# FFN2's last product: seven half-size products over 20 of 22 feature tiles instead of 16, with token sums, weight parts and residuals in a new order

## The chip, the cores and the metric

The kernel runs on 1 core of one Trainium2 chip. The metric is the device time of one execution in microseconds (us); lower is better. Before the change the median of 3 runs is 1121.24 us (1120.5 to 1123.13).

## The reference, cut to what matters

The program is one layer of a streaming encoder: a half-step SwiGLU feed-forward block (FFN1), a mixer, a second half-step feed-forward block (FFN2), and a final RMS norm. Only the end is touched:

```python
def swiglu(h, w1, w3, w2):
    return (jax.nn.silu(h @ w1) * (h @ w3)) @ w2
...
        x = x + 0.5 * swiglu(rms_norm(x, ffn2_norm[l]), ffn2_w1[l], ffn2_w3[l], ffn2_w2[l])
    return rms_norm(x, final_norm)
```

There are 512 tokens, 1024 model columns and 2816 features, all in float32. The change concerns the product with `w2` (512 x 2816 by 2816 x 1024), the residual add and the final norm.

## The kernel before, in words

**Precision.** Every float32 operand is used as two parts: a high part (`hi`, a cast to the matmul's type, on ACT) and a low part (`lo`, the operand minus the high part, on DVE). One product of two operands is then three matmuls: hi by hi, lo by hi, hi by lo.

**The last product.** The features lie in 22 tiles of 128 (`hh[j]`, `hl[j]`: the two parts of tile j, features on partitions, tokens along the row). A *unit* is two neighbouring feature tiles, with a `w2` block of 128 x 2 x 512 (512 KB) for one half of the columns. A matmul takes 128 tokens of a tile as its stationary side and 512 columns of `w2` as its moving side. `ByTokens.run` (L1879) handles 16 tiles in the Strassen-Winograd way: the features are cut in two halves of 4 units (`NU` = 4, `K2` = 8), the tokens in two halves of 256, the columns in two halves of 512, and seven half-size products stand in for eight. Each of the seven has 4 steps, one a unit (`seventh`, L1974), of 12 matmuls. The other 6 tiles (16 to 21) are multiplied plainly (`plainly`, L1984): 48 matmuls for each pair of tiles.

In the text the seven are M1, M2 (plain tokens of the first half by the two feature halves), M5, M6, M3, M7 (with sums of tokens or of weights) and M4. M5 multiplies by the token sum S1, which is written back over the second half of the tokens of `h`; M6, M3 and M7 multiply by the sums S2, S4 and S3. The results collect in eight PSUM banks: X, Y, Z and W of two banks each. Z holds M5 first; `snap` (ACT, L1998) copies it away (`m5`), and then M3 is added to the same bank. X likewise holds M1, then M1 + M6 (`up`), then M7 and M4.

**Weights.** The sums of weight blocks are made by accumulating transfers: `onto` (L1893) lets GpSimd (POOL) issue a transfer from memory that adds to what lies in the buffer. A buffer of the list `chain` holds B11 (M1), then B11 + B12 (M5), then + B22 (M6), then + B21 (M4). An `onto` must wait until the block's present content has been read by both instructions that make its parts, and the next use must wait until it has landed. Plain loads (`fetch`, L1888) go through SP's queue.

**Order.** Everything is emitted in program order and kept so on each engine. `prep` (L1954) makes the two parts of a weight block: a cast on ACT (L1964) and a subtraction on DVE (through `two`, L1903). There are three pairs of buffers for weight parts, used in turn, so the parts of a step can be made once the step three places before it has read its own. `parts` (L1940) makes the two parts of a token sum for M6, M3 and M7, in three buffers in turn. The token sums are made on DVE by `whole`, `s1` and `s234`. In the order before, all four M5 steps come first, then the four M6, four M3, four M7, one plain step, four M4 and the remaining plain tiles; M6's unit u thus uses the buffer `chain[u]` four places after M5's unit u.

**The end.** Each block of 128 tokens gets its last plain matmuls, the residual (read back from `xtok` in memory to `ys`), the sum of squares and the scaling, one block after another, and is stored.

Engines are written PE (matmuls), PEld (loading of the stationary side), DVE, ACT, POOL and SP.

Of the kernel before, what the change touches and what calls it, by code (L numbers as in the profile page):

```python
# [18 lines left out]
P = 128  # L19
# [4 lines left out]
KF = DFF // P  # L24
DA = 512
# [26 lines left out]
def kernel(  # L52
# [658 lines left out]
    def ffn(nrm, w1, w3, w2, nxt, during=(), first=None, seven=None):  # L711
        with tc.tile_pool(name="hp", bufs=1) as hp:
# [9 lines left out]
            def place_h(j):  # L722
                got = []
                if by_tokens and j < 8:
                    if j == 0:
                        firsts.append(hp.tile([P, 8, 2, T], F32R, name="h0to7"))
                    return [firsts[0][:, j, i] for i in range(2)]
# [1124 lines left out]
    class ByTokens:  # L1852
# [5 lines left out]
        def early(s, sv, nrm):  # L1858
            s.sv, s.nrm = sv, nrm

            def scales():
                ps = bank("rst", pr)
                for b in range(NB):
                    keep(pe.transpose(ps[:, b * P:(b + 1) * P], nrm.rstd[:, b * P:(b + 1) * P], ident[:]))
                keep(act.activation(s.small[:, 0:NB], ps[:, 0:T:P], AF.Copy, scale=0.5))

# [12 lines left out]
        def run(s, hh, hl, h, w2, hp):  # L1879
            H, sc, NU = s.H, s.small, 4  # L1880
# [12 lines left out]
            def onto(to, k0, c):  # L1893
                keep(nc.gpsimd.dma_start(to, part(k0, c), accum_op=ALU.add))
# [4 lines left out]
            def mm(ps, a, b, start=False, stop=False):  # L1899
                keep(pe.matmul(ps if isinstance(ps, bass.AP) else ps[:], a, b, start=start, stop=stop, skip_group_check=True))  # L1900

            def two(to, a, b, op=ALU.subtract):
                keep(dve.tensor_tensor(to, a, b, op=op))  # L1903

            chain = [t[:] for t in s.sv.first_raw]
# [6 lines left out]
            S2, S4 = [fp.tile([P, 2 * NU, H], F32, name=f"s{i}", tag=f"O{i}") for i in range(2)]  # L1912
            S3 = [xp.tile([P, 2, H], F32, name="s3", tag="acc", bufs=2)[:] for _ in range(2)]
            S3 += [fp.tile([P, 2, H], F32, name="s3", tag="sq7")[:], xp.tile([P, 2, H], F32, name="s3", tag="rstd")[:]]
            RA, RB = [None] * NU, [None] * NU

            def whole(u):
                ks = slice(2 * u, 2 * u + 2)
                RA[u], RB[u] = unit("E00", name="ra"), unit("E01", name="rb")
                two(RA[u], f32(h[:, ks, 0]), f32(h[:, ks, 1]), ALU.add)  # L1920
                for k in range(2):
                    kk = 2 * NU + 2 * u + k
                    two(RB[u][:, k], f32(hh[kk]), f32(hl[kk]), ALU.add)

            def s1(u):
                v, to = RB[u][:, :, H:T], [h[:, 2 * u:2 * u + 2, i, H:T] for i in range(2)]
                two(v, RA[u][:, :, H:T], v)
                return lambda: keep(act.copy(to[0], v)), lambda: two(to[1], v, f32(to[0]))

            def s234(u):  # L1930
                ks = slice(2 * u, 2 * u + 2)
                two(S2[:, ks], RB[u][:, :, H:T], RA[u][:, :, 0:H])
                two(S3[u], RA[u][:, :, 0:H], RA[u][:, :, H:T])
                two(S4[:, ks], RB[u][:, :, 0:H], S2[:, ks], ALU.add)
# [5 lines left out]
            def parts(S, u):  # L1940
                hi, lo = spots[turn[0] % 3]
                turn[0] += 1
                src = S[u] if isinstance(S, list) else S[:, 2 * u:2 * u + 2]
# [8 lines left out]
            made, done = [2], [0]  # L1952

            def prep(src, own=None):  # L1954
                n = made[0]
                if own:
                    hi, lo = [unit(t, F32R) for t in own]
                else:
                    made[0] += 1
                    if n % 3 == 2:  # L1960
                        hi, lo = fp.tile([P, 2, T], F32R, name="whi", tag="fg")[:], unit("E30", F32R, "wlo")
                    else:
                        hi, lo = [wp.tile([P, 2, T], F32R, tag=t, name=t, bufs=2)[:] for t in ("whi", "wlo")]
                keep(act.copy(hi, src))  # L1964
                two(lo, src, f32(hi))
                if own:
                    return hi, lo
                wide.append((hi, lo))

            def take():  # L1970
                done[0] += 1
                return wide[done[0] - 1]

            def seventh(banks, left, start=False):  # L1974
                hi, lo = take()
# [8 lines left out]
            def plainly(k0, c, ts, start=False):  # L1984
                hi, lo = take()
# [4 lines left out]
                for k in range(2):  # L1990
                    for t in ts:
                        mm(bank_of[t][c], token(hh[k0 + k], t), lo[:, k])
# [12 lines left out]
            prep(chain[2])  # L2005
            whole(0)
            onto(chain[0], 0, 1)
            onto(chain[1], 2, 1)
            seventh(X, plain_h(0, 0), True)
            prep(chain[3])  # L2010
            onto(chain[2], 4, 1)
            onto(chain[3], 6, 1)
            prep(b21[0])
            cast, rest = s1(0)
            seventh(X, plain_h(2, 0))
            prep(b21[1])
            cast()
            f = [fetch(tags[0], 16, 0)]
            s234(0)
            rest()  # L2020
            seventh(X, plain_h(4, 0))
            prep(b21[2])
            f.append(fetch(tags[1], 16, 1))
            whole(1)
            seventh(X, plain_h(6, 0))
            prep(b21[3])
            f.append(fetch(tags[2], 18, 0))
            cast, rest = s1(1)
            seventh(Y, plain_h(K2, 0), True)
            prep(f[0])  # L2030
            cast()
            f.append(fetch(tags[3], 18, 1))
            s234(1)
            rest()
            seventh(Y, plain_h(K2 + 2, 0))
            prep(f[1])
            x0 = snap(X, "x0", 0)
            whole(2)
            seventh(Y, plain_h(K2 + 4, 0))
            prep(f[2])  # L2040
            cast, rest = s1(2)
            seventh(Y, plain_h(K2 + 6, 0))
            prep(f[3])
            cast()
            s234(2)
            rest()
            plainly(16, 0, (0, 1))
            prep(chain[0])
            onto(chain[0], K2, 1)
            whole(3)  # L2050
            plainly(16, 1, (2, 3), True)
            prep(chain[1])
            onto(chain[1], K2 + 2, 1)
            cast, rest = s1(3)
            plainly(18, 0, (0, 1))
            prep(chain[2])
            cast()
            onto(chain[2], K2 + 4, 1)
            plainly(18, 1, (2, 3))
            rest()  # L2060
            s234(3)
            prep(chain[3])
            onto(chain[3], K2 + 6, 1)
            seventh(Z, plain_h(0, 2), True)
            b22 = [fetch(t, K2 + 2 * u, 1) for u, t in enumerate(("E10", "E11", "E00", "E01"))]
            seventh(Z, plain_h(2, 2))
            left = [parts(S2, 0)]
            prep(chain[0])
            seventh(Z, plain_h(4, 2))
# [149 lines left out]
```

## Time and profile before

| what | value |
|---|---|
| median of 3 runs | 1121.24 us (1120.5 to 1123.13) |
| time of the profiled execution | 1121.77 us |
| span of the profiled execution (first to last instruction) | 1120.1 us |
| mean granted clock of TensorE | 0.999 |
| PE busy | 1108.4 us (99%) |
| DVE busy | 911.0 us (81%) |
| ACT busy | 648.8 us (58%) |
| starts of the first and the last matmul of FFN2's last product | 1002.3 us and 1112.4 us |

A profile comes from one execution. The page gives busy times by engine, the chain of work that ended last and the costliest groups of instructions; further views answer for a stretch of time: the timeline of an engine, who waited for whom, busy time by stretch, and transfers with the time from issue to landing. In a timeline row the columns are start, duration, engine, line, operation, what is written from what, count, and in brackets the engine's idle time before it with what ended that. Matmuls overlap: one lasts 0.389 us, and the next begins before it ends.

### The profile page before, as it was taken

The page shows a single profiled execution, that of the slowest core. Times are in us where ns is not written, and L with a number is a line of the kernel's source. Part 1 is how long each engine was busy: PE and PEld are TensorE (multiplying, and loading weights), DVE is VectorE, ACT ScalarE, POOL GpSimd, SP SyncE. Part 2 cuts the span into 40 slices and gives each one's busy share as a digit, 9 for nine tenths or more (in the row PEclk, how much of TensorE's full clock was granted, in tenths as well). Part 3 has the DMA queues.
Part 4 walks back from the last instruction along what each step waited for, and adds up shares of the span by engine and source line. Part 5 has one row for each costly group of instructions (what it writes and reads, how often), then busy time and mean ns, then how long its engine had stood idle before and what let it go on. Part 6 is the DMA issues. An engine that isn't in the chain of part 4 may idle for free.

```text
span 1120.1 us, 19519 instructions
## 1 busy us (share of the span) xinstructions
PE 1108.4 (99%) x7640; PEld 974.3 (87%) x7640; DVE 911.0 (81%) x1429; ACT 648.8 (58%) x1085; POOL 106.1 (9%) x170
## 2 busy tenths in 40 slices
PE   8999999999999999999999999999999999999997
PEld 7899999998887888888777777788999999998786
DVE  6889999988556888768777677878989999989766
ACT  6646555644335954444879768544766655554554
POOL 2000000010000112321000001112000000001220
PEclk9999999999999999999999999999999999999999
DMA  8433333353344343345222236543344433356792
GB/s 264 126 95 105 113 96 113 95 180 114 113 123 119 83 118 110 116 118 140 68 58 74 86 101 194 158 129 95 104 123 126 120 113 96 114 166 172 172 269 105
DMA packets 198218, 139.55 MB, mean 125 GB/s; under 512 B 10574, under 2 KB 178830, under 8 KB 198126
## 3 DMA queue, kind: packets, MB, share of 16 engines
q1 hardware_dynamic: 185854, 110.77, 33.6%
q0 software_dynamic: 10032, 26.74, 9.2%
q8 instruction: 60, 0.98, 0.4%
q10 hardware_dynamic: 2240, 0.79, 0.3%
q14 instruction: 32, 0.26, 0.1%
HBM read 123.41 MB, written 14.88 MB: 123 GB/s over the span
## 4 chain that ended last, share of the span: by engine, by line
PE 92%; issue 3%; DMA 3%; DVE 1%; POOL 0%; ACT 0%; SPq 0%; DVEq 0%; POOLq 0%; ACTq 0%
PE za L142 23%; PE zc L142 14%; PE pgt L142 8%; PE pd L142 6%; PE pk L142 6%; PE ppj L1702 4%; PE pw L142 4%; PE pq L142 4%; PE tx L1900 3%; PE pb L142 3%; PE pa L142 3%; PE pv L142 2%; PE tz L1900 2%; PE pl L142 1%; DMA raw<-in_ffn_w_dram 1%
## 5 line engine op out<-in xcount | busy, mean ns | idle before, releaser
L133 ACT CAST whi<-raw 128x1024 fp32r<-128x1024 f32 (+2 forms) x93 | 90.0, 969 | 104.2 <-issue 16.6
L134 DVE TENSOR_TENSOR wlo<-raw,whi 128x1024 fp32r<-128x1024 f32 (+2 forms) x93 | 104.4, 1123 | 22.5 <-ACT whi L133 22.2
L142 PE MATMUL zc<-xh,wlo 128*128 128x256 f32 x296 | 83.7, 283 | 0.0
L142 PE MATMUL zc<-xl,whi 128*128 128x256 f32 x296 | 83.7, 283 | 0.0
L142 PE MATMUL zc<-xh,whi 128*128 128x256 f32 x296 | 83.7, 283 | 0.0
L142 PE MATMUL za<-e,wtwo 128*128 128x256 f32 x480 | 64.2, 283 | 0.0
L142 PEld LDWEIGHTS za<-e,wtwo 128*128 128x128 f32 x480 | 59.6, 188 | 0.0
L512 ACT CAST wtwo<-wsum 128x1024 fp32r<-128x1024 f32 x37 | 38.9, 1052 | 31.2 <-PE za L142 31.2
L142 PEld LDWEIGHTS zc<-xh,wlo 128*128 128x128 f32 x296 | 56.7, 191 | 0.0
L142 PEld LDWEIGHTS zc<-xl,whi 128*128 128x128 f32 x296 | 56.7, 191 | 0.0
L142 PEld LDWEIGHTS zc<-xh,whi 128*128 128x128 f32 x296 | 56.6, 191 | 0.0
L142 PE MATMUL pgt<-xh,whi 128*128 128x512 f32 x128 | 53.0, 414 | 0.0
L515 DVE TENSOR_TENSOR wlo<-raw,whi 128x1024 fp32r<-128x1024 f32 x41 | 50.0, 1219 | 2.5 <-ACT whi L512 2.5
L524 DVE TENSOR_TENSOR wsum<-wsum,raw 128x512 f32<-128x512 f32 x74 | 50.9, 688 | 1.2
L524 DVE TENSOR_TENSOR wsum<-raw 128x512 f32<-128x512 f32 x74 | 50.7, 685 | 0.0
L142 PE MATMUL pgt<-xh,wlo 128*128 128x512 f32 x128 | 50.1, 391 | 0.0
L142 PE MATMUL pgt<-xl,whi 128*128 128x512 f32 x128 | 50.0, 391 | 0.0
L512 ACT CAST whi<-wsum 128x1024 fp32r<-128x1024 f32 x37 | 38.8, 1049 | 16.7 <-PE zc L142 13.4
L512 ACT CAST whi<-raw 128x1024 fp32r<-128x1024 f32 x41 | 43.1, 1050 | 8.9 <-PE zc L142 7.9
L598 ACT ACTIVATE fs<-fa 128x512 f32<-128x512 f32 x39 | 24.7, 632 | 38.8 <-DVE fa L631 31.6
L515 DVE TENSOR_TENSOR wlo<-wsum,whi 128x1024 fp32r<-128x1024 f32 x37 | 45.1, 1219 | 0.0
L515 DVE TENSOR_TENSOR wtwo<-wsum,wtwo 128x1024 fp32r<-128x1024 f32 x37 | 45.1, 1218 | 0.0
(693 smaller groups left out, 3604.2 us busy)
## 6 DMA issues: line engine op xcount, KB each, us to landing
raw<-in_ffn_w_dram SPq DMA_DIRECT2D x106, 512.0 KB
raw<-in_w_in_dram SPq DMA_DIRECT2D x40, 512.0 KB
wu<-in_ffn_w_dram SPq DMA_DIRECT2D x18, 512.0 KB
raw<-in_ffn_w_dram POOLq DMA_DIRECT2D x12, 512.0 KB, 8.8
raw<-in_w_out_dram SPq DMA_DIRECT2D x8, 512.0 KB
raw<-in_ffn_w_dram SPq DMA_DIRECT2D x8, 384.0 KB
gsave<-gs SPq DMA_DIRECT2D x9, 256.0 KB
xin<-in_x_dram SPq DMA_DIRECT2D x4, 512.0 KB
```

Source lines behind the costliest of these rows:

```text
L133: marks["wide"] = act.copy(hi[:], raw[:])
L134: marks["rest"] = (eng or dve).tensor_tensor(lo[:], raw[:], hi[:].bitcast(F32), op=ALU.subtract)
L142: mm = pe.matmul(ps, w, x_, start=first and n == 0, stop=last and n == 2, skip_group_check=chain)
L512: keep(act.copy(dst, src))
L515: keep(dve.tensor_tensor(dst, src, f32(hi), op=ALU.subtract))
L524: keep(dve.tensor_tensor(to, a, b, op=ALU.add))
L598: keep(act.activation(sa[:], a_[:], AF.Silu))
L1702: keep(pe.matmul(ps[:], a[:, k, :], y[k][b], start=k == 0 and n == 0, stop=k == NP - 1 and n == 2))
L1900: keep(pe.matmul(ps if isinstance(ps, bass.AP) else ps[:], a, b, start=start, stop=stop, skip_group_check=True))
```

## The change

Ten units of two tiles are now handled by the seven products (`KS` = 10 tiles in each feature half, `NU` = 5), and one pair of tiles (20 and 21, `KP` = 20) plainly. The order of the steps is a list, and a table (`plan`) says what is emitted after each step; `ready(n + 3)` emits the parts for the step three places ahead, after the table's row. The steps are numbered from 0: M1 0 to 4, M2 5 to 9, the plain pair's two steps 10 and 11, M5 and M6 12 to 21, M3 22 to 26, M7 27 to 31, a plain step 32, M4 33 to 37, and the last plain step 38.

M5 and M6 are no longer one behind the other as wholes: units 0, 1, 2 of M5, units 0, 1, 2 of M6, then M5 and M6 of unit 3, then M5 and M6 of unit 4. The token sums of unit 4 are prepared by transfers: `sent` copies the high parts of its four tiles inside SBUF (SP's queue), and `joined` adds the low parts (POOL's queue); the buffers that they use (`r0`, `r1`) become those of `up` and `m5` later. The fifth block of `chain` lies in `E10`. Blocks for M3 and M7 (`b22`) are fetched for units 0 to 2 early, and for units 3 and 4 after step 21, since their buffers `E00` and `E01` hold the token sums until then. The residuals are added by accumulating transfers to the saved results (`x0`, `m5`, `up`), and the token blocks 0 and 1 are finished before the last plain step; only blocks 2 and 3 remain for the end.

Line numbers of the changed kernel differ: `onto` is L1897, `two` L1906, `prep`'s cast L2013, `parts`' cast L1999, `snap` L2041.

```diff
+KS = 10
...
-            K2 = 2 * NU
-            tags = ["E10", "E11", "E20", "E21"]
-            b21 = [fetch(tags[u], K2 + 2 * u, 0) for u in range(NU)]
...
-            seventh(Z, plain_h(2, 2))
-            left = [parts(S2, 0)]
-            prep(chain[0])
-            seventh(Z, plain_h(4, 2))
-            left.append(parts(S2, 1))
-            prep(chain[1])
...
+            chain.append(fetch("E10", 8, 0))
...
+            def sent(u):
+                R[u] = [[xp.tile([P, T], F32, name=f"r{n}{i}", tag=f"x{i}{5 + n}")[:] for i in "hl"] for n in range(2)]
+                for n in range(2):
+                    for k in range(2):
+                        kk = n * KS + 2 * u + k
+                        keep(nc.sync.dma_start(over(R[u][n][k], hh[kk]), f32(hh[kk])))
...
+            K2, KP = KS, 2 * KS
+            b21 = [fetch(t, K2 + 2 * u, 0) for u, t in enumerate(("E11", "E20", "E21"))]
+            order = [("M1", u) for u in range(NU)] + [("M2", u) for u in range(NU)] + [("F", 0), ("F", 1)]
+            order += [("M5", 0), ("M5", 1), ("M5", 2), ("M6", 0), ("M6", 1), ("M6", 2), ("M5", 3), ("M6", 3), ("M5", 4), ("M6", 4)]
+            order += [(m, u) for m in ("M3", "M7") for u in range(NU)] + [("L", 1)] + [("M4", u) for u in range(NU)] + [("L", 0)]
...
+            def ready(n):
+                m, u = order[n]
+                if m in ("M6", "M3", "M7"):
+                    made["left", m, u] = parts({"M6": S2, "M3": S4, "M7": S3}[m][u])
+                if n > 1:
+                    prep(source(m, u))
...
+                if m == "M5":
+                    onto(chain[u], part(K2 + 2 * u, 1))
...
+                16: [lambda: s1(4)],
+                17: [lambda: cast(4), lambda: s2(4)],
+                18: [lambda: rest(4)],
+                19: [lambda: s4(3)],
+                20: [lambda: s4(4), fifth_snap],
+                21: [lambda: s3(3), lambda: b22(3, "E00"), lambda: b22(4, "E01")],
+                22: [lambda: s3(4), sixth_snap],
...
+            for n in range(-1, len(order) - 1):
+                if n >= 0:
+                    product(n)
+                for do in plan.get(n, []):
+                    do()
+                if n + 3 < len(order):
+                    ready(n + 3)
```

More of the change, by code (lines that the diff above doesn't have):

```diff
@@ L1921, in whole, with wb @@
+            def wb(u):
                 for k in range(2):
-                    kk = 2 * NU + 2 * u + k
-                    two(RB[u][:, k], f32(hh[kk]), f32(hl[kk]), ALU.add)
-            def s1(u):
[L1926 to L1934, printed above, removed]
+                    kk = KS + 2 * u + k
+                    to = R[u][1][k]
+                    two(over(to, hh[kk]), f32(hh[kk]), f32(hl[kk]), ALU.add)
@@ new lines, in sent, with joined @@
+            def sent(u):
[4 more added lines that the diff above has]
+                        keep(nc.sync.dma_start(over(R[u][n][k], hh[kk]), f32(hh[kk])))
+            def joined(u):
+                for n in range(2):
+                    for k in range(2):
+                        kk = n * KS + 2 * u + k
+                        onto(over(R[u][n][k], hh[kk]), f32(hl[kk]))
@@ new lines, in each, with rows, whole3 @@
+            def each(u, to, a, b, op=ALU.subtract):
+                if len(R[u][0]) == 3:
+                    two(to[2], a[2], b[2], op)
+                else:
+                    for k in range(2):
+                        two(to[k], a[k], b[k], op)
+            def rows(ts, c0):
+                return [t[..., c0:c0 + H] for t in ts]
+            def whole3(t):
+                return [t[:, 0], t[:, 1], t]
+            def s1(u):
+                a21, a22 = rows(R[u][0], H), rows(R[u][1], H)
+                each(u, a22, a21, a22)
@@ new lines, in cast, with rest, s2 @@
+            def cast(u):
+                to, v = h[:, 2 * u:2 * u + 2, 0, H:T], rows(R[u][1], H)
+                if len(v) == 3:
+                    keep(act.copy(to, v[2]))
+                else:
+                    for k in range(2):
+                        keep(act.copy(to[:, k], v[k]))
+            def rest(u):
+                hi, lo = [h[:, 2 * u:2 * u + 2, i, H:T] for i in range(2)]
+                each(u, whole3(lo), rows(R[u][1], H), whole3(f32(hi)))
+            def s2(u):
+                each(u, whole3(S2[u]), rows(R[u][1], H), rows(R[u][0], 0))
@@ L2051, in run @@
-            plainly(16, 1, (2, 3), True)
-            prep(chain[1])
[L2053 to L2065, printed above, removed]
@@ L2111, in run @@
-            seventh(X, plain_h(K2, 2))
-            prep(chain[3])
-            ys = []
-            for t in range(NB):
-                y = wp.tile([P, D], F32, tag="raw", name="yt", bufs=4)[:]
-                keep(nc.sync.dma_start(y, xtok[t * P:(t + 1) * P, :]))
-                ys.append(y)
-            seventh(X, plain_h(K2 + 2, 2))
-            prep(late[1])
-            ends.append(fetch("E21", 18, 0))
-            last = {(18, 1): prep(ends[0], ("E00", "E01"))}
-            seventh(X, plain_h(K2 + 4, 2))
@@ new lines, in ready @@
+            def ready(n):
[4 more added lines that the diff above has]
+                    prep(source(m, u))
+                if m == "M1":
+                    onto(chain[u], part(2 * u, 1))
+                if m == "M5":
+                    onto(chain[u], part(K2 + 2 * u, 1))
+                if m == "M3":
+                    onto(made["b22", u], part(2 * u, 1))
+                    if u == NU - 1:
+                        for v in range(NU):
+                            onto(chain[v], part(K2 + 2 * v, 0))
@@ new lines, in load, with b22, first_snap, fifth_snap @@
+            def load(key, tag, k0, c):
+                made[key] = fetch(tag, k0, c)
+            def b22(u, tag):
+                load(("b22", u), tag, K2 + 2 * u, 1)
+            def first_snap():
+                made["x0"] = snap(X, "x0", 0)
+            def fifth_snap():
+                made["m5"] = snap(Z, "m5", 2)
+            def sixth_snap():
+                made["up"] = snap(X, "up", 0)
+            def c11():
+                for a in range(2):
+                    three(made["x0"][a], Y[a][:], sc[:, a:a + 1], made["x0"][a])
```

339 lines of the change are left out of this document (157 added, 182 removed).

## The prediction

> **What bounds the kernel now.** I read the page, then FFN2's last product by stretches, then the chain of waits there.
>
> ```profile
> span 1120.1 us, 19519 instructions
> PE 1108.4 (99%) x7640; PEld 974.3 (87%) x7640; DVE 911.0 (81%) x1429; ACT 648.8 (58%) x1085; POOL 106.1 (9%) x170
> ```
>
> PE is busy 99% of the span, so a matmul saved is time saved as long as nobody makes PE wait. By stretches (us; busy time and count of PE, PEld, DVE, ACT, POOL; clock, transfers' share, GB/s):
>
> ```profile
> 1010.00:1020.00 10.00, 10.00 (x46) 8.26 (x44) 10.00 (x13) 3.46 (x4) 1.17 (x1) 1.00 1.09 256
> 1020.00:1030.00 10.00, 10.00 (x46) 8.29 (x45) 10.00 (x14) 5.79 (x8) 0.00 (x0) 1.00 0.58 191
> 1030.00:1040.00 10.00, 10.00 (x46) 8.28 (x45) 10.00 (x13) 4.93 (x6) 2.35 (x2) 1.00 0.33 52
> 1050.00:1060.00 10.00, 8.84 (x39) 6.97 (x38) 6.62 (x8) 7.40 (x12) 1.18 (x1) 1.00 0.55 158
> ```
>
> DVE has no slack in the first half; PE falls below 10 only in the last row. The chain of waits (start, us, what) and PE's waits say why:
>
> ```profile
> 1043.68 10.46 DMA raw<-in_ffn_w_dram
> ...
> 1054.22 1.05 ACT whi L1964
> 1055.32 3.04 PE tx L1900 x12
> 1058.36 10.88 PE tz L1900 x48
> ```
>
> ```profile
> PE tx L1900 <- ACT whi L1964: 1.2, 1, 1.2
> ```
>
> An accumulating transfer (`onto`) landed 10.5 us after its issue, ACT's cast of M6's unit 3 waited for it, and PE 1.2 us for the cast: the product's only stall. The row of 48 matmuls gives the pitch, 10.88 / 48 = 0.227 us, so a step of 12 takes 2.72. Without stalls step n starts at 1002.3 + 2.72n. Step 12 (M5) should start at 1034.9, and does:
>
> ```profile
> L1900 PE MATMUL tx<-whi,h0to x32: 389/389/397, 1002.3 to 1012.1; 128*128 128x512 f32 x32
> ...
> L1900 PE MATMUL tz<-whi,h0to x32: 389/389/389, 1035.0 to 1044.7; 128*128 128x512 f32 x32
> ```
>
> **Gains.** Before: 28 steps of the seven and 3 pairs of plain tiles of 48 matmuls, 480. After: 35 x 12 + 48 = 468. Twelve matmuls less are 2.7 us. The 1.2 us stall belongs to the order that is replaced; what is late instead follows. Together -3.9 us.
>
> **The transfer moves between neighbours.** ACT before, from the cast of M5's unit 3 to that of M6's unit 3, both from `raw_10831`, the fourth buffer of `chain`:
>
> ```order
> L1964 CAST whi_11116<-raw_10831 128x1024
> L1944 CAST xh0_7832<-s0_10841 128x2x256
> L1964 CAST whi_11155<-raw_10707 128x1024
> L1944 CAST xh2_7907<-s0_10841 128x2x256
> L1964 CAST whi_11173<-raw_10709 128x1024
> L1944 CAST sph_10847<-s0_10841 128x512
> L1964 CAST whi_11191<-raw_10829 128x1024
> L1998 ACTIVATE m50_11195<-tz0_10837,small_8117 128x512
> L1998 ACTIVATE m51_11197<-tz1_10838,small_8117 128x512
> L1944 CAST xh0_7832<-s0_10841 128x2x256
> L1964 CAST whi_11213<-raw_10831 128x1024
> ```
>
> ACT after, from M5's unit 3 to the copy of bank Z (`m50`); `raw_10828` and `wu_10830` are the fourth and fifth buffers:
>
> ```order
> L2013 CAST whi_11199<-raw_10828 128x1024
> L1999 CAST xh0_7832<-s0_10840 128x2x256
> L2013 CAST whi_11220<-raw_10828 128x1024
> L1977 CAST h0_8201<-r1h_10924 128x256
> L1977 CAST h0_8201<-r1l_10925 128x256
> L2013 CAST whi_11240<-wu_10830 128x1024
> L1999 CAST xh2_7907<-s_10842 128x2x256
> L2013 CAST whi_11261<-wu_10830 128x1024
> L1999 CAST sph_10849<-s1_10841 128x512
> L2013 CAST whi_11280<-wu_11039 128x1024
> L2041 ACTIVATE m50_11299<-tz0_10836,small_8117 128x512
> ```
>
> Nine rows stood between the two casts of a buffer; now one does, in unit 3 and in unit 4. In between, DVE must read the old content, POOL issue the `onto`, and the data land. ACT works in order: while M6's unit 3 waits, M5's unit 4 waits behind it, so the second transfer can't start during the first wait. The prices:
>
> ```profile
> 999.69 0.42 DVE L524 TENSOR_TENSOR gate<-gate,za 128x256 f32<-128x256 f32 x1 [3.00 <-PE za L142]
> 1000.03 1.22 DVE L515 TENSOR_TENSOR wlo<-raw,whi 128x1024 fp32r<-128x1024 f32 x1
> 1001.16 0.68 DVE L524 TENSOR_TENSOR fa<-fa,zc 128x512 f32<-128x512 f32 x1
> 1001.88 0.69 DVE L631 TENSOR_TENSOR fa<-fa,rstd 128x512 f32<-128x512 f32 x1
> ...
> 1006.01 1.22 DVE L1903 TENSOR_TENSOR wlo<-raw,whi 128x1024 fp32r<-128x1024 f32 x1
> 1007.14 1.22 DVE L1903 TENSOR_TENSOR ra<-h0to 128x1024 f32<-128x1024 f32 x1
> ...
> 1013.49 0.69 DVE L1903 TENSOR_TENSOR s<-rb,ra 128x512 f32<-128x512 f32 x1
> 1014.09 0.69 DVE L1903 TENSOR_TENSOR s<-ra 128x512 f32<-128x512 f32 x1
> ...
> 1033.41 1.22 DVE L1903 TENSOR_TENSOR wlo<-raw,whi 128x1024 fp32r<-128x1024 f32 x1
> ```
>
> ```profile
> 1034.93 1.17 POOL L1894 DMA_DIRECT2D raw<-in_ffn_w_dram  x1 [22.76 <-DVE wlo L1903]
> ```
>
> ```profile
> raw<-in_ffn_w_dram POOLq DMA_DIRECT2D x1, 512.0 KB, 5.8
> ```
>
> From start to start DVE takes 1.13 us for a low part, 0.60 at 512 wide, 0.34 at 256, and 0.12 more where an instruction needs the one just before (1001.16 to 1001.88). POOL starts 0.3 after DVE's end (1034.63 to 1034.93). With no other load in flight the data land 5.8 us after the issue.
>
> **Place one, unit 3 (step 19).** Up to the end of this block's low part DVE has 21 wide instructions (17 low parts, 4 token sums) and 29 of 512 (8 sums of `hh` and `hl`, 18 for S1 to S4 and S1's low parts, 3 low parts of S2): 21 x 1.13 + 29 x 0.60 = 41.1 from 1006.0, so 1047.1 to 1048.3 with ten dependent pairs. Add 0.1, POOL's 0.3, 5.8 and the cast's 1.05: 1054.4 to 1055.6, against 1054.0 for step 19. Stall 0.4 to 1.6. It grows if the weights of M2 and the plain pair come late, since DVE then loses time: in SP's queue `sent` puts four copies between two of these loads, and POOL's `joined` adds four accumulations beside them. A load beside accumulations took 8.2 us, from its issue at 1011.86 to the cast that waited for it:
>
> ```profile
> 1011.86 67.68 SPq L1890 DMA_DIRECT2D wu<-in_ffn_w_dram  x13
> ```
>
> ```profile
> 1020.01 1.05 ACT L1964 CAST whi<-wu 128x1024 fp32r<-128x1024 f32 x1 [3.71 <-DMA wu<-in_ffn_w_dram]
> ```
>
> At this price the block for step 8, issued when step 5's low part is done (about 1015.6), is cast by 1024.9, 0.8 after step 8's start at 1024.1, and three more blocks follow. I take 2.3 for all this, bounds 0.4 and 6.
>
> **Place two, unit 4 (step 21).** Counted from the end of step 19's cast: DVE's low part 1.13, two S2 halves 0.34 each with 0.1, the low part for step 20 until its end 1.22, POOL 0.3, transfer 5.8, cast 1.05, handovers 0.2: 10.5. Two steps cover 5.4. Stall 5.0. Nothing else loads then; with the 10.5 us row in place of 5.8 it would be 9.7. Bounds 4.9 and 9.7. [...]
>
> **Place three, bank Z (step 22).** M3 adds to the bank that `m50` must copy after M5's unit 4. Four M6 steps used to lie between; now one does. DVE after the change, from step 21's low part on:
>
> ```order
> L1906 TENSOR_TENSOR wlo_11262<-wu_10830,whi_11261 128x1024
> L1906 TENSOR_TENSOR s1_10841<-rb_11118,s0_10840 128x512
> L1906 TENSOR_TENSOR spl_10850<-s1_10841,sph_10849 128x512
> L1906 TENSOR_TENSOR wlo_11281<-wu_11039,whi_11280 128x1024
> L1906 TENSOR_TENSOR s_10843<-r1h_10924,s_10842 128x256
> L1906 TENSOR_TENSOR s_10843<-r1l_10925,s_10842 128x256
> ```
>
> `m50` is written over `r1h`, so ACT's copy waits for both last rows: 1.13 + 0.60 + 0.60 + 1.13 + 0.8 = 4.3 after step 21's cast, and 0.6 for the copy (1.25 for two):
>
> ```profile
> 1050.05 1.25 ACT L1998 ACTIVATE m<-tz,small 128x512 f32<-128x512 f32 x2
> ```
>
> With handovers 5.0, of which step 21 covers 2.7. Stall 2.3, bounds 2.1 and 2.5.
>
> **Place four, `b22`'s unit 3 (step 25).** `E00` is free only when S3's unit 3 is made: after step 22's start ACT's second copy and a token part (1.1), DVE's low halves and low part (0.6, 1.4 with its cast) and S3 (0.6) make about 4.0. A plain 512 KB took 5.0 in the nearest row, where little else moved:
>
> ```profile
> fgain<-in_final_norm_dram POOLq DMA_DIRECT2D x1, 512.0 KB, 5.0
> ```
>
> 4.0 + 5.0 + 1.1 = 10.1 against three steps, 8.2: 1.9; with 8.2 for the load 5.1; SP's issue is shorter, so none is possible too. I take 1.5, bounds 0 and 5.1. M4's blocks have seven steps (19 us) and need no term.
>
> **The end.** Rows of before:
>
> ```profile
> 1112.38 0.39 PE L1900 MATMUL tw<-wlo,hh 128*128 128x512 f32 x1
> ```
>
> ```profile
> 1114.11 0.16 DVE L2179 SCALAR_TENSOR_TENSOR small<-small 128x1 f32<-128x1 f32 x1 [0.18 <-ACT junk L2168]
> ...
> 1115.45 0.87 DVE L2188 SCALAR_TENSOR_TENSOR yt<-yt,small,fgain 128x256 f32<-128x256 f32 x2
> ```
>
> ```profile
> 1116.46 0.90 SPq L2189 DMA_DIRECT2D out_dram<-yt  x2
> ```
>
> ```profile
> L298 DVE TENSOR_SCALAR xh<-xT,par x4: 479/487/489, 5.9 to 15.3; 128x512 fp32r<-128x512 f32 x4
> ```
>
> PE ends at 1112.8, the last store is issued by 1117.4, the span ends at 1120.1: 7.3. After: until 1114.3 the same, then two products with the gain (1.2) and three scalings (about 1.4): DVE ends 4.1 after PE instead of 3.5, but one store is issued behind it instead of two: 0 within 0.3. The two `up` residuals, queued on POOL behind M4's five transfers, may hold DVE up to 1.3. I take 0.3, bounds -0.3 and 1.3.
>
> **Sum.** -3.9 + 2.3 + 5.0 + 2.3 + 1.5 + 0.3 = +7.5 us. The profiled execution's 1121.8 (span 1120.1 and 1.7 around it) becomes 1129.3; it lies 0.5 above the median of 1121.2, so the predicted median is 1128.7.
>
> **Rivals.** (a) *Covered after all, faster*: the transfers land before ACT asks, only the gains stay, 1121.2 - 3.9 = 1117.3. For: units 0 to 2 keep three steps. Against: unit 4's would have to land in 0.7 us (5.4 less the 4.7 of the other items). Chance 0.10. (b) *Waits overlap*: only place two costs, 1121.2 - 3.9 + 4.9 = 1122.2. Against: the four waits follow one another on ACT and DVE. 0.07. (c) *The clock falls*. PE idle for 4.0 us at the end lost half its clock (us; clock, share, GB/s behind PE's busy time):
>
> ```profile
> 1114.00:1115.00 1.00, 0.00 (x0) 1.00 0.40 156
> 1115.00:1116.00 1.00, 0.00 (x0) 1.00 0.00 0
> 1116.00:1117.00 1.00, 0.00 (x0) 0.88 0.61 231
> 1117.00:1118.00 1.00, 0.00 (x0) 0.50 0.97 359
> ```
>
> Place two's 5.0 is split by step 20, which runs inside it, so about 4 is one piece, at the edge. One step at half clock costs 2.7 more: 1131.4. [...] 0.12. (d) *The loads bound the first half*: place one at 6, 1128.7 + 3.7 = 1132.4. 0.13.
>
> **Numbers.** The forecast itself gets 0.58. Below 0.2% (2.2 us, about what a measurement can tell) counts as no change: (b). Faster 0.10, same 0.07, slower 0.58 + 0.12 + 0.13 = 0.83. The range reaches from (b), 1122.2, to places one and four at their upper bounds, 1128.7 + 3.7 + 3.6 = 1136.0; outside are (a) and the tails.
>
> **What would show it.** In the changed profile: PE waiting for ACT's cast (`whi`) before step 19 and for about 4 us before step 21, with ACT waiting there for transfers into `raw` and `wu`; PE or its `tz` matmuls waiting for `m`'s copy; POOL waiting for `wlo` ahead of each. PE busy 99% without these waits would make it wrong.

## The result, and the profile after

The changed kernel takes 1137.26 us (median; 1136.52 to 1139.53), the kernel before on the same chip 1121.03 us (1120.5 to 1123.13): a ratio of 1.0145, with a 95% interval of 1.0125 to 1.0164. It is 16.2 us slower; forecast were 7.5, with 1136.0 as the upper end. The first lines of the page after:

```profile
span 1136.0 us, 19554 instructions
PE 1112.2 (98%) x7628; PEld 974.6 (86%) x7628; DVE 914.5 (80%) x1439; ACT 651.7 (57%) x1092; POOL 119.4 (11%) x183
```

PE has 12 matmuls fewer (7640 before) and yet 3.8 us more of busy time, and the span is 15.9 us longer. From here on *product* is the time from the first matmul of FFN2's last product to the end of its last one, and *end* what the span has behind that.

| | before | after | difference |
|---|---|---|---|
| first matmul starts at | 1002.29 | 1001.42 | -0.87 |
| product | 110.48 | 125.14 | +14.66 |
| end | 7.29 | 9.44 | +2.15 |

The start is not the change's: over the runs below it varies from 1000.8 to 1003.0.

PE's waits in the product of the changed kernel (total, times, longest; us):

```profile
PE tx L1903 <- ACT whi L2013: 7.6, 3, 4.1
PE tz L1903 <- ACT whi L2013: 3.1, 2, 2.5
PE ty L1903 <- ACT whi L2013: 1.0, 1, 1.0
PE tz L1903 <- ACT m L2041: 0.4, 1, 0.4
```

Before there was one, of 1.2. The first matmuls of the product, and of the steps 19, 21, 22 and 26, on PE's timeline:

```profile
1001.42 1.78 PE L1903 MATMUL tx<-whi,h 128*128 128x512 f32 x7
...
1059.62 0.79 PE L1903 MATMUL tx<-whi,xh 128*128 128x512 f32 x1 [4.08 <-ACT whi L2013]
...
1069.79 0.80 PE L1903 MATMUL tx<-whi,xh 128*128 128x512 f32 x1 [3.11 <-ACT whi L2013]
...
1074.53 0.50 PE L1903 MATMUL tz<-whi,sph 128*128 128x512 f32 x1 [0.36 <-ACT m L2041]
...
1089.22 0.50 PE L1903 MATMUL tz<-whi,xh 128*128 128x512 f32 x1 [2.55 <-ACT whi L2013]
```

At 2.72 a step, step 19 should start 51.7 after the first matmul and starts 58.2 after it: place one is 6.5. From 19 to 21 it takes 10.17 instead of 5.44: place two, 4.7. From 21 to 22 4.74 instead of 2.72: place three, 2.0. From 22 to 26 14.69 instead of 10.88: place four, 3.8. ACT's timeline says what the casts waited for:

```profile
1021.43 1.05 ACT L2013 CAST whi<-wu 128x1024 fp32r<-128x1024 f32 x1 [4.87 <-DMA wu<-in_ffn_w_dram]
1025.96 1.04 ACT L2013 CAST whi<-wu 128x1024 fp32r<-128x1024 f32 x1 [2.96 <-DMA wu<-in_ffn_w_dram]
...
1031.56 1.06 ACT L2013 CAST whi<-wu 128x1024 fp32r<-128x1024 f32 x1 [3.22 <-DMA wu<-in_ffn_w_dram]
...
1058.52 1.04 ACT L2013 CAST whi<-raw 128x1024 fp32r<-128x1024 f32 x1 [7.52 <-DMA raw<-in_ffn_w_dram]
...
1068.69 1.04 ACT L2013 CAST whi<-wu 128x1024 fp32r<-128x1024 f32 x1 [6.54 <-DMA wu<-in_ffn_w_dram]
...
1082.56 1.05 ACT L2013 CAST whi<-wu 128x1024 fp32r<-128x1024 f32 x1 [0.30 <-DMA wu<-in_ffn_w_dram]
...
1088.12 1.04 ACT L2013 CAST whi<-wu 128x1024 fp32r<-128x1024 f32 x1 [4.00 <-DMA wu<-in_ffn_w_dram]
```

The first three are plain loads (M2's last two blocks and the plain pair's second), late from step 8 on. 1058.52 and 1068.69 are the casts for steps 19 and 21, each waiting for the `onto` that refills the buffer of the step just before. The last two are `b22`'s units 3 and 4. Behind the long waits the clock is at half, here in the steps 19, 21 and 26 (us; busy time and count of PE, PEld, DVE, ACT, POOL; clock, transfers' share, GB/s):

```profile
1060.00:1062.00 2.00, 2.00 (x6) 1.52 (x6) 2.00 (x4) 1.60 (x3) 0.00 (x0) 0.50 0.01 4
...
1070.00:1072.00 2.00, 2.00 (x5) 1.63 (x6) 2.00 (x3) 1.21 (x2) 0.00 (x0) 0.50 0.00 0
...
1090.00:1092.00 2.00, 2.00 (x6) 1.52 (x6) 2.00 (x4) 2.00 (x3) 1.28 (x2) 0.50 0.78 144
```

The last row belongs to step 26, which takes 4.4 instead of 2.7. With 1.6 for that, the parts are 6.5 + 4.7 + 2.0 + 3.8 + 1.6 = 18.6, of 18.9 that the product takes over its matmuls' pitch; before it was 1.5. 18.9 - 1.5 - 2.7 (the twelve matmuls) = 14.7, the product's difference. (In place three PE waits only 0.36 us, because step 21 itself runs at half clock and covers the rest; in the run with zero matmuls below, where it runs at full clock, PE waits 1.72 us there and the step takes as long, 4.74.)

The end has a cause of its own. The transfers' engines from 1083 us on, before (to 1115) and after (to 1122.5), in 40 slices, tenths busy, with the queue of the accumulating transfers (packets, MB, share) and landings:

```profile
DMA  9999999999896951000000000000007900069052
...
q0 software_dynamic: 166, 0.55, 5.6%
```

```profile
DMA  9999999952799999999999999999999999999999
...
q0 software_dynamic: 3205, 6.11, 85.8%
...
x<-xtok POOLq DMA_DIRECT2D x2, 256.0 KB, 23.1
...
up<-xtok POOLq DMA_DIRECT2D x2, 256.0 KB, 10.4
```

Before, this stretch had almost no accumulating transfers (M4's were issued by 1071). After, M7's last two blocks, M4's five and six residuals go through one queue there. `up`'s residuals land 10.4 us after their issue at 1112.60, about 1123, and DVE's row shows what follows: the four scalings of the finished blocks stand ahead of the final two blocks. PE's last matmul for the first of these two ends at 1125.2; DVE comes to it at 1126.78.

```profile
1124.12 0.75 DVE L1909 SCALAR_TENSOR_TENSOR x<-x,small,fgain 128x512 f32<-128x512 f32 x1 [0.99 <-ACT small L2139]
...
1126.78 1.53 DVE L1909 SCALAR_TENSOR_TENSOR yt<-tx,small,yt 128x512 f32<-128x512 f32 x3
```

### The profile page after: what moved, and what is told of

It reads as the page before. It is cut to its first block, busy times and chain, and to the rows that moved or that the text cites. A ratio compares the mean times of both kernels' runs of the same rounds, so it can differ in the third digit from the quotient of the medians.

```text
span 1136.0 us, 19554 instructions
## 1 busy us (share of the span) xinstructions
PE 1112.2 (98%) x7628; PEld 974.6 (86%) x7628; DVE 914.5 (80%) x1439; ACT 651.7 (57%) x1092; POOL 119.4 (11%) x183
## 4 chain that ended last, share of the span: by engine, by line
PE 88%; issue 5%; DMA 3%; DVE 2%; POOL 1%; ACT 1%; SPq 0%; DVEq 0%; POOLq 0%; ACTq 0%
PE za L143 23%; PE zc L143 14%; PE pgt L143 8%; PE pd L143 6%; PE pk L143 6%; PE ppj L1703 4%; PE pw L143 4%; PE pq L143 4%; PE pb L143 3%; PE pa L143 3%; PE pv L143 2%; DMA wu<-in_ffn_w_dram 1%; PE tx L1903 1%; PE pl L143 1%; DMA up<-xtok 1%
```

## The experiments

The theory: the loss is a chain of data waits, at the neighbours on one `chain` buffer (units 3 and 4), at bank Z and at `b22`'s late fetch, with late loads ahead. Its rivals: the loads alone; the falling clock; transfers too many in all. All twelve runs, each beside the kernel before on the same chip (us; product and end from the profiled execution, which lies within 1.8 us of the median, but 2.2 above it for the second combination). The diffs below show the rows that an edit changes, not all that it takes out:

| kernel | median | ratio to before, 95% | product | end |
|---|---|---|---|---|
| changed kernel | 1137.26 | 1.0145 (1.0125 to 1.0164) | 125.1 | 9.4 |
| neighbours spread | 1130.15 | 1.0081 (1.0066 to 1.0096) | 116.9 | 10.6 |
| unit 4's copies three steps later | 1138.98 | 1.0159 (1.0144 to 1.0175) | 124.9 | 10.9 |
| zero matmuls in the waits | 1138.97 | 1.0157 (1.0142 to 1.0172) | 123.9 | 11.2 |
| `b22` fetched early | 1135.39 | 1.0126 (1.0110 to 1.0143) | 121.7 | 9.8 |
| two residuals early | 1136.19 | 1.0130 (1.0113 to 1.0147) | 125.9 | 7.9 |
| without unit 4's transfers | 1135.21 | 1.0128 (1.0113 to 1.0143) | 120.7 | 10.9 |
| combined, first | 1130.94 | 1.0085 (1.0070 to 1.0100) | 117.4 | 7.9 |
| combined, second | 1126.38 | 1.0056 (1.0043 to 1.0068) | 117.5 | 7.9 |
| the second, with the neighbours | 1133.85 | 1.0112 (1.0096 to 1.0127) | 123.7 | 7.9 |
| combined, third | 1123.73 | 1.0019 (1.0010 to 1.0028) | 109.6 | 10.3 |
| combined, fourth | 1121.39 | 1.0001 (0.9992 to 1.0010) | 108.5 | 10.5 |
| combined, fifth | 1119.37 | 0.9985 (0.9976 to 0.9994) | 108.5 | 8.9 |

The changed kernel was not timed again beside the others, and the intervals of five single edits overlap its own. For those the reading rests on the trace, not on the median.

**The neighbours spread.**

```diff
-("M6", 0), ("M6", 1), ("M6", 2), ("M5", 3), ("M6", 3), ("M5", 4), ("M6", 4)
+("M6", 0), ("M5", 3), ("M6", 1), ("M6", 2), ("M5", 4), ("M6", 3), ("M6", 4)
```

> The changed kernel (1137.3 us) with one line altered: M5's unit 3 is computed between M6's units 0 and 1, and M5's unit 4 ahead of M6's unit 3, so that the two products that share a chain buffer stand four steps (unit 3) and two steps (unit 4) apart instead of one, and one more step lies between M5's last unit and M3. Nothing else is changed. Theory of the neighbours (a buffer whose content is cast, read, refilled and cast again within one step): place two falls from 4.7 to about 2.0 us (10.2 us of turnaround against three steps, 8.2), place three from 2.0 to 0, and place one keeps only what the late loads cost (3 to 5 of 6.5); a half-clock stretch may go with it. Together 6 to 9 us less: 1128 to 1131. If the loads of the first half were the cause of nearly everything: 2 us less or no change, 1135 to 1137. If the falls of the clock were what costs, and any wait of 2.6 us or more sets one off: as many remain as there are such waits, 1131 to 1135.

Measured 1130.15, 7.1 less; the product is 8.3 shorter, the end longer. PE's waits:

```profile
PE tz L1903 <- ACT whi L2013: 3.1, 2, 2.7
PE tz L1903 <- DVE h L1906: 2.6, 1, 2.6
PE ty L1903 <- ACT whi L2013: 2.4, 2, 1.4
```

The wait for `tx` (places one and two) is gone, and bank Z with it. What is left is `b22` (3.1), the late loads (2.4), and a new wait for unit 3's token sum, which M5's unit 3 now needs sooner. The measured time lies in the range of the theory of the neighbours; the loads alone can't explain it, since nothing about them was altered.

**The loads.** First the copies only moved:

```diff
-                2: [..., lambda: sent(4)],
+                5: [..., lambda: load(("F", 1), "E11", KP, 1), lambda: sent(4)],
-                6: [..., lambda: joined(4)],
+                7: [..., lambda: joined(4)],
```

> The changed kernel with the four copies that SP issues between two loads (sent) put behind the plain pair's second load, three steps later, and POOL's accumulations on them (joined) one step later. Theory of the late loads (the loads for steps 8, 9 and 11 come late since the copies stand in their queue, DVE then idles for 3.5 us, and place one is late by as much): place one 3 to 4 us shorter, 1133 to 1134.5. Theory of the turnaround alone (place one is late since DVE has that much work, the loads don't matter): within 1 us of 1137.3. If the copies only move to where other loads are issued: as late as before or later, 1137 to 1139.

Measured 1138.98, no gain, as the third expectation had it. Steps 8 to 14 then ran without any wait, but the accumulations of `joined` stood ahead of M6's first `onto` in the queue: step 15 waited 3.1, and step 19 started 59.0 after the first matmul (58.2 before the edit). Moving them showed only that they collided again at their new place. So they were left out:

```diff
-                        keep(nc.sync.dma_start(over(R[u][n][k], hh[kk]), f32(hh[kk])))
+                        keep(nc.gpsimd.memset(over(R[u][n][k], hh[kk]), 0.0))
...
-                        onto(over(R[u][n][k], hh[kk]), f32(hl[kk]))
+                        pass
```

> The changed kernel without the transfers that make the token sums of unit 4 (four copies and four accumulations, 2 MB): their buffers are filled with zeros by POOL instead, so the sums of unit 4 are left out and the result is not the reference's. Nothing takes these transfers' place in the queues, unlike in the kernel that only moved them. Theory that they make the first half late (1.5 us of waits at steps 8 to 11, 3.7 us that DVE idles there, and thereby 3 to 5 of place one's 6.5): those waits go, step 19 starts 3 to 5 us earlier after the start of the product, and the time is 1132.5 to 1134.5. Theory that place one is the turnaround of the buffer alone: steps 8 to 11 without waits, but step 19 as late as before within 1 us, 1136 to 1137. The forecast of the prediction for place one without late loads was 0.4 to 1.6 us.

Measured 1135.21, between the two ranges. Steps 8 to 18 have no wait at all, and step 19 starts 55.3 after the first matmul (1056.68 - 1001.36): 2.9 earlier, and still 3.6 late. So place one's 6.5 is 2.9 of late transfers and 3.6 of turnaround. The second number is the surprise. DVE's waits in the product of this run up to 1056 us, all ahead of step 18's low part:

```profile
DVE wlo L1906 <- ACT whi L2013: 1.3, 2, 0.7
DVE wlo L1906 <- PE tx L1903: 1.1, 1, 1.1
```

and on ACT, the cast for step 15 (M6's unit 0, three steps behind M5's) and that for step 19:

```profile
1039.59 1.05 ACT L2013 CAST whi<-raw 128x1024 fp32r<-128x1024 f32 x1 [4.65 <-DMA raw<-in_ffn_w_dram]
...
1055.59 1.04 ACT L2013 CAST whi<-raw 128x1024 fp32r<-128x1024 f32 x1 [7.43 <-DMA raw<-in_ffn_w_dram]
```

Three steps don't hide the refill of unit 0 either: PE doesn't wait for it, but ACT does (4.65), and DVE behind ACT (2.4 in all, 1.8 of it behind the casts for M6's units 0 and 1), and so step 18's low part, which frees the buffer for step 19, ends at 1049.7. That this wait of ACT's is what delays DVE is read from the trace; no run removed it alone. The product is 4.4 shorter here, the median only about 2: the end grew to 10.9.

**The clock.** Ahead of steps 19, 21 and 26, matmuls with a weight tile of zeros:

```diff
+                if n in (19, 21, 26):
+                    idle(*{19: (X[0], 16), 21: (X[0], 12), 26: (Z[0], 9)}[n])
```

> The changed kernel with matmuls that add nothing (a weight tile of zeros) ahead of steps 19 (16 of them), 21 (12) and 26 (9), into the bank that the step adds to, so that PE is busy while it waits for its weights and the granted clock stays at full. The three stretches at half clock took 4.4 us over their pitch. If a fall of the clock costs its whole price: 4.4 us less, 1133. If the first two lie inside a wait that the next cast ends anyway, as the trace of the changed kernel suggests: only the third counts, 1.6 us less, 1135.7. If the padding is longer than the wait: up to 1 us more than that.

```profile
1060.00:1062.00 2.00, 2.00 (x10) 1.50 (x8) 2.00 (x5) 1.14 (x2) 0.00 (x0) 1.00 0.01 4
...
1076.00:1078.00 2.00, 2.00 (x6) 1.51 (x6) 2.00 (x3) 1.11 (x2) 0.79 (x1) 0.50 0.98 177
...
1090.00:1092.00 2.00, 2.00 (x10) 1.66 (x9) 2.00 (x4) 2.00 (x3) 1.28 (x2) 1.00 0.27 50
```

Measured 1138.97, above all three expectations. The clock stayed at 1.00 in the three stretches (first and third row). Step 26 then took 2.85 instead of 4.45: 1.6. But the steps 19 to 21 took 9.9 against 10.2, since a cast that waits for a transfer ended that stretch at either clock, and step 21 took 4.74 in both, since PE now waits 1.7 us for the copy of bank Z. A fall elsewhere (1074.7 to 1078, second row) made step 22 1.6 longer; 0.85 of that is left at step 26, the rest went into the wait for `b22`. So here a fall cost 1.6 where no data wait stood behind it, and next to nothing where one did; of the changed kernel's three, one counts. The product came out 1.3 shorter, the median not: `up`'s residual left at the same time in both kernels.

```profile
1112.60 1.73 POOL L1897 DMA_DIRECT2D up<-xtok  x2 [1.01 <-DVE up L1909]
```

```profile
1112.61 1.72 POOL L1899 DMA_DIRECT2D up<-xtok  x2 [2.22 <-DVE up L1911]
```

**`b22` early.**

```diff
+                16: [lambda: s1(4), lambda: s4(3)],
+                17: [lambda: cast(4), lambda: s2(4), lambda: s3(3)],
+                18: [lambda: rest(4), lambda: b22(3, "E00"), lambda: b22(4, "E01")],
-                19: [lambda: s4(3)],
...
-                21: [lambda: s3(3), lambda: b22(3, "E00"), lambda: b22(4, "E01")],
```

> The changed kernel with S4's and S3's units 3 made three to four steps earlier in the plan, and the loads of the last two blocks of b22 issued from step 18 on instead of 21. Theory of the late fetch (the loads for steps 25 and 26 start only when S3's unit 3 has freed their buffers): place four's 3.8 us go, and the half clock behind them, 1.6: together 5.4 less, 1132. If the two sums, now in DVE's and ACT's queues ahead of the casts for steps 19 and 21, delay those: up to 2.5 of it comes back, 1132 to 1134.5. If the loads are slow for another reason: within 1 us of 1137.3.

Measured 1135.39, 0.9 above the second range. PE's waits for `tz` are gone:

```profile
PE tx L1903 <- ACT whi L2013: 8.3, 2, 4.2
PE ty L1903 <- ACT whi L2013: 1.5, 2, 1.1
```

Steps 23 to 38 run at their pitch; place four (3.8) and the half clock behind it (1.6) are gone. The loads now run beside the `onto` for step 21, whose cast waits 7.97 instead of 6.54, and place two grows from 4.7 to 6.2. The product is 3.5 shorter, the end 0.4 longer.

**Residuals early.** `x0`'s and `up`'s:

```diff
+                18: [lambda: residual("x0", 0, 0), lambda: rest(4)],
...
+                23: [lambda: residual("up", 0, 1)],
-                24: [c11, lambda: residual("x0", 0, 0)],
...
-                33: [c12, lambda: residual("up", 0, 1)],
```

> The changed kernel with two of the three residuals issued earlier on POOL's queue: x0's after step 18 instead of 24 (the transfers' engines are a third busy there) and up's after step 23 instead of 33 (up is saved with its sign turned, so that the residual can be added first); m5's stays. In the changed kernel the transfers' engines are busy without a gap from 1083 to 1122 us, x0's residual needs 23 us to land, up's, the last in the queue, 10, and the end behind the last matmul is 2.1 us longer than before. Theory of the full queue at the end (up's landing sets when the two finished blocks leave DVE, and that when the last two can start): the end falls back by 1.5 to 2.1 us, 1135 to 1136. Theory that ACT and DVE have that much more work after the last matmul, whatever lands: no change, 1137. If the early residuals hold back the transfers for steps 22 to 26: the end is shorter, but place four grows by as much, 1136.5 to 1138.

Measured 1136.19, between the first range and the third. The end falls from 9.4 to 7.9, so it is the full queue that made it late: DVE now stands ready for the first of the final two blocks and waits for PE.

```profile
1125.98 0.75 DVE L1909 SCALAR_TENSOR_TENSOR yt<-tx,small,yt 128x512 f32<-128x512 f32 x1 [0.68 <-PE tx L1903]
```

The product is 0.7 longer, but not for the reason in the third expectation: steps 22 to 26 take 14.63 us (14.69 before the edit). The clock stays at half for 6.8 us there instead of 3.4 (1088.1 to 1094.9), and the steps 26 and 27 take 1.3 more.

**All of it, and the neighbours once more.** The first combination, with M5's unit 3 between M6's units 1 and 2:

```diff
+("M6", 0), ("M6", 1), ("M5", 3), ("M6", 2), ("M5", 4), ("M6", 3), ("M6", 4)
...
+                10: [lambda: sent(4), lambda: cast(2), lambda: s3(2), lambda: s4(2)],
...
+                13: [lambda: joined(4), lambda: s1(3)],
...
+                18: [lambda: residual("x0", 0, 0), lambda: rest(4), lambda: b22(3, "E00"), lambda: b22(4, "E01")],
+                21: [lambda: residual("m5", 2, 1)],
...
+                23: [lambda: residual("up", 0, 1)],
```

> All that the runs so far speak for, together: M5's unit 3 between M6's units 1 and 2 and M5's unit 4 between M6's 2 and 3 (the kernel with unit 3 one place earlier waited 2.6 us there for its token sum); the four copies for unit 4's sums after step 10 and their accumulations after step 13, where the transfers' engines have room; S4's and S3's units 3 and the last two blocks of b22 early; all three residuals early. If the places are what the traces show and add up: place one 0 to 2, two 0 to 1, three 0, four 0 to 1, the end as before (7.3) and 12 matmuls saved, 1117.5 to 1122, thus the same as or faster than the kernel before (1121.2). If the transfers only collide elsewhere (they are a fifth more in total than before): 1123 to 1130, and a wait for a late load at another step.

1130.94: the hope failed; the time is 0.9 above the other range, and the waits came back elsewhere as that one had it. Steps 0 to 16 ran without a wait, but unit 4's low token part stood on DVE behind a weight part that waited for a transfer (2.9 at step 19), and M7's last `onto` behind two residuals (2.4 at step 31). The second mends these:

```diff
+                17: [lambda: cast(4), lambda: rest(4), lambda: s3(3)],
...
+                25: [lambda: residual("up", 0, 1)],
...
+                35: [c12, lambda: square_of("x0", 0), lambda: square_of("x0", 1)],
```

> The kernel that combined the edits (1130.9 us), with its three remaining waits taken up: unit 4's low token part is made one place earlier on DVE, ahead of a weight part that waits for a transfer (2.9 us at step 19, and 1.8 of half clock behind it); up's residual is queued behind M4's five accumulations instead of ahead of M7's last one (2.4 us at step 31 and what follows at 32 and 33, 5.8 with the half clock); DVE adds M3's part to up two places later. If these are the causes: 1.3 us of excess over the pitch is left where there were 11.1, the end stays at 8 us: 1119 to 1122. If the transfers' engines, which are a fifth busier than in the kernel before, are the bound: the waits move to steps 33 to 37, 1123 to 1128.

1126.38, in the second range: unit 4's two waits are gone, but 1.7 us at step 15, 2.6 at step 21 and 2.1 at step 33 (DVE late with `m5`, behind a weight part that waits for a transfer) came in their place. (The profiled execution took 1128.62, 2.2 above the median.) Beside it the same kernel with the changed kernel's order of steps, and nothing else altered:

> The kernel of the run beside this one, word for word, but with the changed kernel's order of the ten steps: M5's and M6's unit 3 next to each other, and unit 4's. All loads, sums, fetches and residuals stand as they do there, so the two runs differ by the neighbours alone. Theory of the neighbours: place one 2 to 3.6 (the turnaround without late loads, as the run without unit 4's transfers had it), place two about 4.7, place three about 2, one half-clock stretch: 7 to 11 us slower than the run beside it. If late loads and the order of transfers are the cause instead and the neighbours only show where the loss ends up: within 3 us of the run beside it.

1133.85, 7.5 more. PE's waits for casts, first of the spread kernel, then with the neighbours:

```profile
PE tx L1903 <- ACT whi L2013: 4.3, 2, 2.6
```

```profile
PE tx L1903 <- ACT whi L2013: 8.2, 3, 3.8
```

Two pairs of kernels that differ by the order of ten steps alone, 7.1 and 7.5 apart, the second on one chip with intervals far from touching: that is the price of the neighbours. In the first pair bank Z's place is part of it (step 21 takes 4.7 us with the neighbours, 2.8 spread); in the second step 21 takes 4.45 in both. The third to the fifth follow the waits that are left:

```diff
+                6: [lambda: sent(4), lambda: cast(1), lambda: s3(1), lambda: s4(1)],
...
+                17: [lambda: s1(4), lambda: cast(4), lambda: s4(3), lambda: rest(4), lambda: s3(3)],
...
+                20: [lambda: s4(4), fifth_snap, lambda: residual("x0", 0, 0)],
...
+                26: [lambda: c22(W, sc), c11],
...
+                31: [lambda: c22(X, neg)],
```

> The spread kernel with all edits (1126.4 us, of which the profile shows 11.3 us of excess over the matmuls' pitch: 1.9 at step 15, 2.8 and 1.7 of half clock at step 21, 2.3 and 1.9 at step 33), with those three taken up. The four copies for unit 4 stand behind the plain pair's second load again, but their accumulations stay late; DVE makes step 19's low part ahead of unit 4's sums, and x0's residual goes behind the transfer for step 21 by one more place; the second addition of M7's part to m5 stands one place earlier, ahead of a weight part that waits for a transfer. If each wait has the cause that its trace names: 2 to 4 us of excess left, 1118 to 1121, thus level with or a little faster than the kernel before (1121.0). If the transfers as a whole are the bound, the waits come back elsewhere: 1123 to 1127.

1123.73, above the 1121 that was hoped for and in the second range. The product fell to 109.6, below before's 110.5, but the end went back to 10.3. The next edit takes `x0`'s residual, now in the full queue, for the cause.

```diff
+                18: [lambda: residual("x0", 0, 0), lambda: s2(4), lambda: b22(3, "E00"), lambda: b22(4, "E01")],
+                19: [lambda: s4(4)],
+                20: [fifth_snap],
```

> The last combined kernel (1123.7 us; its product takes 109.6 us from the first matmul to the last, 0.9 less than the kernel before, but the end behind it takes 10.4 instead of 7.3) with two rows of the table moved: x0's residual right behind the transfer for step 21, where the transfers' engines run dry at 1058 us, instead of into the full queue that ends at 1107; S4's unit 4 one place earlier on DVE, ahead of a weight part, since the copy of bank Z waits for it (1.4 us at step 22). If the full queue is what makes the end late (M4's last block, up's residual, the addition that waits behind both): the end falls to 8 to 8.5, the product by 1 to 2: 1119 to 1121, level with the kernel before or up to 0.2% faster. If not: 1122 to 1124.

1121.39, between the two ranges and level with before. The product is 108.5; the end did not come down (10.5), so `x0`'s residual was not what made it late. DVE still waited 2.8 for the cast of M4's last block, with 7.7 us of work behind that (1102.98 to 1110.67), and came to the final two blocks 1.2 after PE's last matmul:

```profile
1102.98 1.23 DVE L1906 TENSOR_TENSOR wlo<-wu,whi 128x1024 fp32r<-128x1024 f32 x1 [2.77 <-ACT whi L2013]
...
1110.67 1.52 DVE L1909 SCALAR_TENSOR_TENSOR yt<-tx,small,yt 128x512 f32<-128x512 f32 x3
```

```diff
+                33: [lambda: square_of("x0", 0), lambda: square_of("x0", 1)],
+                34: [others],
+                35: [c12],
```

> The last combined kernel (1121.4 us, level with the kernel before; its product is 2.0 us shorter than before's, its end behind the last matmul 3.1 longer) with the squares of x0 and m5 and m5's product with the gain issued one to two steps earlier, where DVE waits 2.8 us for M4's last block, instead of behind that wait. If DVE's row of work behind that block sets the end: 1.3 to 1.8 us less, 1119.6 to 1120.2. If the stores or ACT's chain set it: no change, 1121.4.

1119.37 beside 1120.9, 0.2 below the range: faster than the kernel before by 0.15% (0.06 to 0.24%). The end is 8.9, 1.5 less, with the product unchanged, so that 1.5 was DVE's row of work. PE's waits that are left:

```profile
PE tx L1903 <- ACT whi L2013: 0.4, 1, 0.4
PE tz L1903 <- DVE h L1906: 0.3, 1, 0.3
PE tx L1903 <- DVE m L1909: 0.2, 1, 0.2
```

This kernel still makes every transfer of the changed kernel, and takes 18 us less. So it is not the number of transfers that costs, but where they stand, with the order of the steps.

## Why the prediction was wrong

The direction was right, and the mechanism in the main; the size was not: 16.2 instead of 7.5, from terms that were mis-sized.

- **Gains**, forecast 3.9, measured 4.2 (2.7 for the matmuls, 1.5 for the old stall and what went with it). Right.
- **Place one**, forecast 2.3 with bounds 0.4 and 6, measured 6.5. This is the step that failed first. It counted DVE's instructions up to step 18's low part as a row without gaps. In the run without unit 4's transfers that part ended 48.3 after the first matmul, where the forecast had 44.8 to 46.0; the 2.4 that DVE waited for casts and buffers is the difference from the upper figure. 1.8 of it stands behind the refill of unit 0, which the forecast took as covered by three steps. So the turnaround alone cost 3.6 and not 0.4 to 1.6, and the late loads, for which the forecast had added about 1, cost 2.9.
- **Place two**, forecast 5.0, measured 4.7, and **place three**, 2.3 and 2.0: right, by the same items; the half clock that falls into both adds next to nothing, as the zero matmuls showed (9.9 against 10.2 us for the steps 19 to 21, and 4.74 for step 21 in both). The transfer took 5.8 (issued at 1062.92, cast at 1068.69), as the quoted row had it.
- **Place four**, forecast 1.5 with bounds 0 and 5.1, measured 3.8. The step costed unit 3's fetch alone. Unit 4's goes through the same queue behind it, and its wait (2.55 on PE) is the larger.
- **The end**, forecast 0.3 with an upper bound of 1.3, measured 2.1. The step named the queue ahead of the `up` residuals but bounded its price at 1.3 without a row of such a queue. All that the change makes accumulating goes through that queue, and moving two residuals out of its full stretch took 1.5 off.
- **The clock** stood as rival (c) and not in the sum. It fell three times; one fall counts, 1.6. The prediction's estimate of 2.7 took a whole step at half clock; step 26 had 3.4 us at half clock (1089.77 to 1093.18) and took 4.45, against 2.85 at full clock in the run with zero matmuls.
- **The rivals as alternatives.** (c) and (d) were given the chances of other worlds, each added alone to the forecast. They came true together, beside it (the loads with 2.9 of place one's 6.5): their causes are the same full queue and the same waits. The range, built from the upper bounds of places one and four alone, ended 1.3 short; it had left out the end's own upper bound and the clock.

By size, what the forecast missed is place one (4.2), place four (2.3), the end (1.8) and the clock (1.6).

What stays open: in five of the six single edits the end grew by 0.4 to 1.8, and gave back some or all of the product's gain. That the queue sets it was shown by the early residuals (1.5), that DVE's row does by the last combination (1.5); how the two share the end in the other runs was not tried.

## What to carry to other kernels

Where one buffer is cast, read, refilled by an accumulating transfer and cast again, cost the round (here 10.2 us) against the steps between the two uses, for all pairs and not only for the closest: a wait that PE doesn't see can still delay the engines that feed the next pair (here, as the trace reads, 4.65 us on ACT and behind it 1.8 on DVE). When an edit turns loads into accumulating transfers, add up what the one queue holds by stretch, to the end of the kernel, and put transfers that nobody awaits into the stretch where it runs dry (here two residuals moved out of its full stretch took 1.5 us off the end). Terms that share a queue are not alternatives; add them.

## What the runs showed of the hardware

The idle time of PE alone didn't tell whether the clock fell. It fell after 4.08, 3.11 and 2.55 us in the changed kernel, and in the run with zero matmuls after 1.72 us (ahead of step 22), but not after 2.72 us in the run with the neighbours spread. What made the difference was not tried. The rows below show the third fall of the changed kernel, whose wait ends at 1089.22, the fall in the run with zero matmuls, whose wait ends at 1073.67, and the run with the neighbours spread behind its 2.72 us, which end at 1082.18:

```profile
1088.00:1090.00 2.00, 0.78 (x3) 0.69 (x4) 0.80 (x1) 1.88 (x3) 0.00 (x0) 0.94 1.14 207
1090.00:1092.00 2.00, 2.00 (x6) 1.52 (x6) 2.00 (x4) 2.00 (x3) 1.28 (x2) 0.50 0.78 144
...
1074.00:1074.50 0.50, 0.50 (x3) 0.25 (x2) 0.00 (x0) 0.50 (x2) 0.00 (x0) 1.00 0.00 0
1074.50:1075.00 0.50, 0.50 (x3) 0.35 (x3) 0.26 (x1) 0.50 (x2) 0.00 (x0) 0.72 0.33 49
1075.00:1075.50 0.50, 0.50 (x3) 0.40 (x2) 0.43 (x1) 0.50 (x1) 0.00 (x0) 0.50 1.20 143
...
1082.00:1084.00 2.00, 1.82 (x8) 1.53 (x9) 1.84 (x3) 2.00 (x4) 0.32 (x1) 1.00 1.12 206
1084.00:1086.00 2.00, 2.00 (x10) 1.39 (x9) 2.00 (x4) 1.84 (x4) 2.00 (x4) 1.00 0.37 46
```

In the changed kernel the clock was at half from 1059.05, 1069.29 and 1089.77, each time for 3.4 us.

What an accumulating transfer took depended here on what stood in the queue with it: 512 KB took 5.8 us alone (issued at 1062.92, cast at 1068.69; nothing else was moved in between), and 256 KB took 23.1 us behind M4's five blocks.
